# Strassen's seven block products for eight in the gate and up projections of the long sequence, with the stages in a new order and the residual gathered in DRAM

## The chip, the cores and the metric

The kernel runs on one core of one Trainium2 chip. The metric is the device time of an execution in microseconds; a lower time is better. The core has a matrix engine (TensorE, "PE" in the profile, with "PEld" for its weight loads), a vector engine (DVE), a scalar engine (ACT), a general engine (POOL) and a sync engine (SP). Work is kept in SBUF (on-chip memory, 128 partitions) and matmuls accumulate in PSUM banks, which hold 128 x 512 fp32 each. DMA queues move data between DRAM and SBUF; here SP issues the loads of weights, and POOL issues everything that is written to DRAM and read back.

## The reference, cut to what matters

One encoder layer is applied to a long sequence ("s", 1024 tokens) and a short one ("p", 512 tokens), each of width 1024, with the same weights. Per sequence a modulation vector scales and shifts the input of each of the three sub-layers:

```
mod = silu(c) @ w_ada + b_ada                      # 9 vectors of 1024: shift, scale, gate three times
hn = rmsnorm(x, ffn1_norm) * (1 + sc1) + sh1
x = x + 0.5 * g1 * swiglu(hn, w_gate, w_up, w_down)    # silu(hn @ w_gate) * (hn @ w_up) @ w_down
hn = rmsnorm(x, mix_norm) * (1 + sc2) + sh2
q, k, v, hy_in = split(hn @ w_in)
x = x + g2 * (concat(rmsnorm(attention(q, k, v)), rmsnorm(hyena(hy_in))) @ w_out)
hn = rmsnorm(x, ffn2_norm) * (1 + sc3) + sh3
x = x + 0.5 * g3 * swiglu(hn, w_gate2, w_up2, w_down2)
y = rmsnorm(x, final_norm)
```

The hidden width of each feed-forward network is 2816, 22 blocks of 128 columns. Attention is a neighbourhood attention over a grid 64 wide; hyena convolves the sequence with filters that a small network makes, once for each sequence length.

## The kernel before, in words

Activations are kept transposed: x of a sequence is a list of chunks of 512 tokens (`q.xT[c]`, two chunks for the long sequence, one for the short), each 8 tiles of 128 features by 512 tokens. Every matrix product is done in fp32r with both operands split into a high half (a copy rounded to fp32r, on ACT) and a low half (the rest, on DVE), and three terms: high by high, low by high, high by low. `mm` (L130) issues a matmul, `load_unit` (L347) loads a 512 KB piece of weights and splits it into halves, `col_unit` (L360) does so for one block of 128 columns.

`ffn` (L519) is a feed-forward network. It goes over 11 groups of two column blocks. For a column block it makes gate and up of each chunk, 8 k-tiles x 3 terms = 24 matmuls of 128x512 for each of the two; ACT takes silu, DVE multiplies, and the product is split into halves again. `down` then multiplies the two blocks by their rows of w_down: 8 output tiles of 6 matmuls for each chunk. DVE adds each output tile, times the gate, into x, which stays in SBUF. For the long sequence that is 192 + 96 = 288 matmuls a group, for the short one 144, with six loads of 512 KB in both cases.

The order of the work is set by `merge` (L1224). It takes a main stream (matrix products) and a side stream (filters, hyena, attention), and lets the side stream advance in step with the main one, by counters of TensorE and DVE work, against totals in the table `PLAN`. Operations of the main stream are recorded at L116 and of the side stream at L118, DMAs at L152 (SP) and L155 (POOL). The stages are:

- A: the first network of the long sequence, with the filters of the long sequence, the rest of the modulation vectors (`ada_rest`, 24 loads of 1 MB into `wada6a` and `wada6b`) and the filters of the short sequence as side work
- C: the projection of the long sequence, the first network and the projection of the short one, with the hyena and the attention of the long sequence as side work
- E: the output projection and the second network of the long sequence, with the attention and hyena of the short one, and its output projection, as side work
- last, the second network of the short sequence alone

Names in the profile: `gu`, `dn` and `mx` are PSUM banks (3, 2 and 3 of them), `hl` halves of weights, `raw` the weights as loaded, `act` activations, `s` and `a` small tiles of 128x512 (two buffers each), `hn1h` and `hn1l` the halves of the modulated input, `xTs` or `xRs` the resident x of the long sequence, `xscr_s` its place in DRAM, `mscA` and `mscB` scratch, `qscr`, `kscr`, `hscr` and `vscr` places in DRAM.

Of the kernel before, what the change touches and what calls it, by code (L numbers as in the profile page):

```python
# [17 lines left out]
P = 128  # L18
# [74 lines left out]
def build(ctx, tc, nc, A):  # L93
# [107 lines left out]
    for qn, L in SEQ_LEN.items():  # L201
# [5 lines left out]
        q.C = L // 512  # L207
        q.x = A[f"x_{qn}"]
# [389 lines left out]

    def proj_v(q, hn):

        vv = q.vscr.rearrange("(a b) c -> b a c", b=q.R)
        for cc in range(2):
# [6 lines left out]
            for b in range(q.R):  # L609
# [13 lines left out]
    def proj_qk(q, hn, part, hps, dst=None):  # L623
# [11 lines left out]
        for c in range(q.C):  # L635
# [31 lines left out]
    def proj_hy(q, hn, bk):  # L667
# [5 lines left out]
        for c in range(q.C):  # L673
# [258 lines left out]
    def hyena(q, ar, mc):  # L932
# [11 lines left out]
        for cb in range(NCB):  # L944
# [34 lines left out]
            for c in range(q.C):  # L979
# [3 lines left out]
                if mc is None:  # L983
                    se.copy(x[:, c * 512:(c + 1) * 512], ps)
                else:
                    se.copy(mc[c][4 + cb], ps)
            if mc is None:
                dmb(q.mscr[cb], x)
# [190 lines left out]
    class Final:  # L1179
# [6 lines left out]
        def add(self, c, kt):  # L1186
# [4 lines left out]
            if kt == 0 and self.q is Pq:  # L1191
                se.activation(warm, self.sq[c].acc[:, 0:1], AF.Sqrt)
# [75 lines left out]
    xr = [slices(i, "xr", F32) for i in (6, 7)]  # L1268
    rs = []
# [7 lines left out]
    def x_in(c, get):  # L1277
        ss = t_st()
        load_x(S, c, c, blk(2 + c, [P, 4, 1024], F32, "xin"), ss, junk, get)
        rs.append(rstd_rows(rstd_cols(ss, D)))  # L1280

    def x_scale(c, kts):
        for kt in kts:
            tt(xr[c][kt], S.xT[c][:, kt], rs[c], ALU.mult)
    x_in(0, gu)
    x_scale(0, range(KT))
# [3 lines left out]
    x_in(1, dn)  # L1290
    hn1 = [hn_pair(2, 3, "hn1"), hn_pair(4, 5, "hn1")]
    norm_pre(S, hn1, 0, xr[0], lo4)
    filS = filters(S, 7, *mixed_msc())

    def begin1():
        sums = [(gu(), gu()), (gu(), dn())]
        gemm_along(sums[0], w0, *hn1[0], lo4)
        x_scale(1, lo4)
        norm_pre(S, hn1, 1, xr[1], lo4)
        gemm_along(sums[1], w0, *hn1[1], lo4)  # L1300
        x_scale(1, hi4)
        ada_half(1, get_ring)
        norm_pre(S, hn1, 0, xr[0], hi4)
        gemm_along(sums[0], w0, *hn1[0], hi4)
        norm_pre(S, hn1, 1, xr[1], hi4)
        gemm_along(sums[1], w0, *hn1[1], hi4)
# [19 lines left out]
    hn2 = []  # L1326

    def after1(c, sq):
        hn2.append(hn_pair(2 + 2 * c, 3 + 2 * c, "hn2"))
        norm_mod(S, 1, hn2, c, sq)  # L1330

    side = chain(filS, ada_rest, lambda: filters(Pq, 7, *mixed_msc()))
# [18 lines left out]
    def s_attention():  # L1351
        kT = [blk(i, [P, 4, 1024], F32R, "kTs") for i in (4, 5)]
        for i in range(2):
            for h in range(4):
                dmb(kT[i][:, h], S.khl[4 * i + h])
# [203 lines left out]
```

## Time and profile before

| | us |
|---|---|
| median of 3 runs | 3217.09 (3212.54 to 3219.84) |
| the profiled execution, its own time | 3219.08 |
| span of the profile, first to last instruction | 3217.2 |
| TensorE busy | 3167.9 |
| DVE busy | 1940.6 |
| ACT busy | 1082.3 |
| POOL busy | 237.5 |

The profiled execution is one execution on the chip. A busy time is the union of an engine's instructions; a group's own busy time can count overlapping instructions apart, so that the mean of a matmul in a group is longer than the time from one matmul to the next. "Idle before" is the time in which the engine stood still just before an instruction of the group, and the arrow says what ended that.

### The profile page before, as it was taken

The numbers are of one execution on the slowest core, as the hardware profiler recorded it, in microseconds if no ns is written. First come the engines' busy times: TensorE is split into PE (matmuls) and PEld (weight loads), VectorE is DVE, ScalarE is ACT, GpSimd is POOL, SyncE is SP. The second block draws the span as 40 slices with busy tenths as digits, with TensorE's granted clock in tenths as the row PEclk, the third lists the DMA queues.
The fourth block names the chain that finished last, engine by engine and source line by source line (L and its number), as shares of the span: only waits on it lengthen the run. The fifth ranks groups of instructions, "written<-read, shape, count | busy, mean of one in ns | idle before, by whom it ended". The sixth has DMA issues, their size and how long they took to land.

```text
span 3217.2 us, 40525 instructions
## 1 busy us (share of the span) xinstructions
PE 3167.9 (98%) x15819; PEld 2592.3 (81%) x15819; DVE 1940.6 (60%) x3537; ACT 1082.3 (34%) x1964; POOL 237.5 (7%) x417
## 2 busy tenths in 40 slices
PE   7999999999999999999999999999999999999998
PEld 5788887778887889887777877788888888888887
DVE  5777653336784856987667468556554444654545
ACT  5211111112254333224666456411122222543233
POOL 1000030000111012001221000000000000000000
PEclk9999999999999999999999999999999999999999
DMA  7222154331354355434443444222111222343332
GB/s 263 88 78 78 55 171 162 131 124 54 89 173 138 124 151 180 168 111 145 127 131 123 151 137 136 84 63 76 58 58 46 66 85 85 118 131 99 99 95 76
DMA packets 320559, 364.09 MB, mean 113 GB/s; under 512 B 13536, under 2 KB 271736, under 8 KB 313488
## 3 DMA queue, kind: packets, MB, share of 16 engines
q1 hardware_dynamic: 287808, 232.81, 23.6%
q0 software_dynamic: 32528, 128.69, 12.5%
q8 instruction: 124, 2.03, 0.3%
q14 instruction: 67, 0.55, 0.1%
q10 hardware_dynamic: 32, 0.01, 0.0%
HBM read 310.33 MB, written 60.51 MB: 115 GB/s over the span
## 4 chain that ended last, share of the span: by engine, by line
PE 90%; issue 4%; DVE 2%; DMA 2%; ACT 1%; POOL 0%; SPq 0%; DVEq 0%; POOLq 0%; ACTq 0%
PE gu L130 56%; PE dn L130 20%; PE mx L130 13%; PE mx L134 1%; PE dn L134 1%; DVE r L118 1%; DMA xin<-in_x_s 0%; DMA mscA<-qscr_s 0%; DVE fT6b L118 0%; DMA mscr_s<-hyz6b 0%; DVE fA6a L118 0%; DMA raw<-in_w_in 0%; PE gu L134 0%; DMA fT6b<-in_zt_p 0%; DMA raw<-in_ffn_w_up 0%
## 5 line engine op out<-in xcount | busy, mean ns | idle before, releaser
L116 ACT ACTIVATE hl<-raw 128x512 fp32r<-128x512 f32 x680 | 427.6, 631 | 1023.3 <-PE gu L130 476.9
L116 DVE TENSOR_TENSOR hl<-raw,hl 128x512 fp32r<-128x512 f32 x680 | 465.2, 689 | 460.8 <-ACT hl L116 458.4
L130 PE MATMUL dn<-act,hl 128*128 128x512 f32 x2904 | 695.0, 393 | 3.5 <-DVE xTp L116 3.5
L130 PEld LDWEIGHTS dn<-act,hl 128*128 128x128 f32 x2904 | 539.1, 188 | 130.2 <-issue 5.7
L130 PE MATMUL gu<-hn3h,hl 128*128 128x512 f32 x1408 | 438.9, 392 | 0.0
L130 PE MATMUL gu<-hn1h,hl 128*128 128x512 f32 x1392 | 434.5, 392 | 0.8 <-ACT hn1h L116 0.8
L130 PEld LDWEIGHTS gu<-hn1h,hl 128*128 128x128 f32 x1392 | 258.1, 188 | 67.5 <-issue 9.1
L130 PEld LDWEIGHTS gu<-hn3h,hl 128*128 128x128 f32 x1408 | 262.9, 188 | 56.8 <-issue 3.4
L116 DVE TENSOR_TENSOR a<-s,gu 128x512 f32<-128x512 f32 x131 | 90.0, 687 | 331.1 <-PE gu L130 331.1
L130 PE MATMUL gu<-hn3l,hl 128*128 128x512 f32 x704 | 274.7, 390 | 0.0
L130 PE MATMUL gu<-hn1l,hl 128*128 128x512 f32 x696 | 271.5, 390 | 0.0
L130 PE MATMUL gu<-hn1ph,hl 128*128 128x512 f32 x704 | 224.9, 394 | 1.1 <-DVE hl L116 1.1
L130 PE MATMUL gu<-hn3ph,hl 128*128 128x512 f32 x704 | 217.4, 389 | 0.0
L130 PE MATMUL gu<-hn2h,hl 128*128 128x512 f32 x640 | 201.6, 395 | 2.8 <-ACT hl L116 2.6
L116 ACT ACTIVATE s<-gu 128x512 f32<-128x512 f32 x132 | 79.0, 598 | 340.6 <-PE gu L130 340.4
L116 DVE SCALAR_TENSOR_TENSOR xTs<-dn,Gc_s,xTs 128x512 f32<-128x512 f32 x176 | 131.5, 749 | 53.4 <-PE dn L130 52.6
L116 DVE SCALAR_TENSOR_TENSOR xRs<-dn,Gc_s,xRs 128x512 f32<-128x512 f32 x176 | 131.7, 749 | 45.3 <-PE dn L130 44.9
L130 PEld LDWEIGHTS gu<-hn3l,hl 128*128 128x128 f32 x704 | 132.2, 188 | 27.7 <-issue 0.5
L130 PEld LDWEIGHTS gu<-hn1ph,hl 128*128 128x128 f32 x704 | 130.9, 188 | 29.0 <-issue 2.6
L130 PEld LDWEIGHTS gu<-hn3ph,hl 128*128 128x128 f32 x704 | 132.1, 188 | 27.5
L130 PEld LDWEIGHTS gu<-hn1l,hl 128*128 128x128 f32 x696 | 130.7, 188 | 29.0 <-DVE hn1l L116 0.8
L116 ACT ACTIVATE act<-a 128x512 fp32r<-128x512 f32 x132 | 83.4, 632 | 193.6 <-DVE a L116 190.5
(393 smaller groups left out, 4553.1 us busy)
## 6 DMA issues: line engine op xcount, KB each, us to landing
raw<-in_ffn_w_gate SPq DMA_DIRECT2D x92, 512.0 KB, 4.0
raw<-in_ffn_w_up SPq DMA_DIRECT2D x92, 512.0 KB, 4.0
raw<-in_ffn_w_down SPq DMA_DIRECT2D x92, 512.0 KB, 3.5
raw<-in_w_in SPq DMA_DIRECT2D x48, 512.0 KB, 4.2
wada6b<-in_w_ada SPq DMA_DIRECT2D x12, 1024.0 KB, 4.9
wada6a<-in_w_ada SPq DMA_DIRECT2D x12, 1024.0 KB, 4.9
raw<-in_w_out SPq DMA_DIRECT2D x24, 512.0 KB, 4.2
kscr_s<-fA6a POOLq DMA_DIRECT2D x8, 1024.0 KB, 4.6
```

The costliest lines, as they stand in the source:

```text
L116: return fn(*a, **k)
L118: r = fn(*a, **k)
L130: nc.tensor.matmul(out, lhsT, rhs, start=start, stop=stop)
L134: nc.tensor.transpose(out, in_, idn)
```

## The change

- `Fast` and `Pair` do gate and up of the long sequence with Strassen's scheme (in Winograd's form) over 2 x 2 blocks: two column blocks of the weights, two halves of the 1024 features, two chunks of tokens. Seven products of 512 features replace eight, `PRODUCTS` lists them. `A` blocks are the weights, `S` blocks sums of them (made anew in each group, on DVE); `B` blocks are activations, `T` blocks sums of them (made once for a network, when `need` first asks).
- `ffn_fast` runs a network of the long sequence with these. A PSUM bank goes on accumulating after ACT has copied its value out, so that the intermediate sums come out of the bank.
- In `down`, all groups but the last send their output tile to DRAM: ACT multiplies it by the gate into a tile `s` or `a`, and a DMA with an addition (`accum_op`) adds it to `xscr_s`. The x of the long sequence is no longer resident in a network; the last group reads it back and adds on DVE as before.
- The stages are in a new order. A: the first network and the projection of the short sequence, with the filters, `ada_rest` and the input of the long sequence (`s_input`) as side work. Then the first long network alone. C: the long projection, with attention and hyena of the short sequence. D: the output projection and second network of the short sequence, with hyena and attention of the long one. Then the long output projection and the second long network, alone.
- The short attention takes q and k as halves in fp32r, as the long one did, for fp32 before.

The core of the diff:

```diff
-    def mm(out, lhsT, rhs, start, stop):
+    def mm(out, lhsT, rhs, start, stop, resume=False):
         work["pe"] += size(rhs) * (0.42 if rhs.dtype == F32R else 1.68)
-        nc.tensor.matmul(out, lhsT, rhs, start=start, stop=stop)
+        nc.tensor.matmul(out, lhsT, rhs, start=start, stop=stop, skip_group_check=resume)
...
+    PRODUCTS = (("A11", "B11"), ("S1", "T1"), ("S2", "T2"), ("A12", "B21"), ("S3", "T3"), ("S4", "B22"),
+                ("A22", "T4"))
...
+        def need(self, nm):
+            if nm in self.T:
+                return
...
+            for i in range(4):
+                if nm == "B11":
+                    self.scale(0, i)
+                    self.split(nm, i, z1[i], self.b1[i])
+                elif nm == "T1":
+                    self.scale(1, i)
+                    tt(z1[i], z2[i], z1[i], ALU.subtract)
+                    self.split(nm, i, z1[i], None)
...
+        def weights(self, nm):
+            a, t = self.A, self.tmp
+            if nm == "S1":
+                tt(t, a["A21"], a["A22"], ALU.add)
+                h = self.halves(t)
+                tt(a["A21"], a["A11"], a["A21"], ALU.subtract)
+                tt(a["A11"], t, a["A11"], ALU.subtract)
+                a["S3"], a["S2"] = a["A21"], a["A11"]
+                return h
...
+        def product(self, n, T):
+
+            b = self.banks
+            (wh, wl), (th, tl) = self.weights(PRODUCTS[n][0]), T
+            to, start = ((0, True), (2, True), (0, False), (1, True), (0, False), (2, False), (0, False))[n]
+            if b[to] is None:
+                b[to] = self.get()
+            for i in range(4):
+                mm(b[to], wh[i], th[i], start and i == 0, False, not start)
+                mm(b[to], wl[i], th[i], False, False, not start)
+                mm(b[to], wh[i], tl[i], False, i == 3, not start)
+            k = self.keep
+            if n == 0:
+                se.copy(k[0], b[0])
+            elif n == 1:
+                se.copy(k[3], b[2])
+            elif n == 2:
+                se.copy(k[1], b[0])
+            elif n == 3:
+                tt(k[0], k[0], b[1], ALU.add)
+            elif n == 4:
+                se.copy(k[2], b[0])
+                tt(k[2], k[2], k[3], ALU.add)
+            elif n == 5:
+                tt(k[1], k[1], b[2], ALU.add)
...
+            G = Pair(wg, f0, [t_raw(), t_raw()], mA[:, 1024:1536], [None] * 3, keeps[0])
+            U = Pair(wu, f0, [t_raw(), mB], mA[:, 1024:1536], [None] * 3, keeps[1])
+            G.get, U.get = gu, mx
+            for n, (_, b) in enumerate(PRODUCTS):
+                fast.need(b)
+                for pr in (G, U):
+                    pr.product(n, fast.T[b])
+                if end and n < 2:
+                    if n == 0:
+                        q.xT = []
+                    reload_x(q, n, xblocks[n])
+                yield
...
+                    if end:
+                        xv = q.xT[c][:, dt]
+                        stt(xv, ps, gain, xv, ALU.mult, ALU.add)
...
+                    else:
+                        y = (t_s, t_a)[dt % 2]()
+                        se.activation(y, ps, AF.Copy, scale=gain)
+                        nc.gpsimd.dma_start(q.xscr[c][:, dt * 512:(dt + 1) * 512], y, accum_op=ALU.add)
...
+    merge("A", p_front(), chain(filters(Pq, 7, *mixed_msc()), ada_rest,
+                                lambda: filters(S, 7, *mixed_msc()), s_input))
...
+    run(ffn_fast(S, fast[0], A["ffn1_w_gate"], A["ffn1_w_up"], A["ffn1_w_down"], 0, after1, None, 7, (0, 5)))
...
+    merge("C", s_proj(), p_mixer())
...
+    merge("D", p_back(), s_mixer())
...
+        if c == 0:
+            fast.append(Fast(S, 2, z3, rows3, {"B11": 0, "T1": 1, "T2": 4, "B21": 6, "T3": 2, "B22": 3, "T4": 5}))
+            for nm in ("B11", "B21"):
+                fast[1].need(nm)
...
+    run(ffn_fast(S, fast[1], A["ffn2_w_gate"], A["ffn2_w_up"], A["ffn2_w_down"], 2, None,
+                 Final(S, any_ps, lambda c, b: t_act()), 7, (0, 1)))
...
-PLAN = {"A": (976e3, 446e3, 0.0, 0.92), "C": (952e3, 413e3 + 40e3, 0.0, 0.94), "E": (1116e3, 250e3 + 15e3, 0.0, 0.93)}
+PLAN = {"A": (726e3, 509e3, 0.0, 0.94), "C": (321e3, 176e3, 0.0, 0.94), "D": (586e3, 413e3, 0.0, 0.94)}
```

The order of TensorE in the first long network, before: gate of one column block, in runs of three terms for each k-tile, with matmuls of the filters (`mx<-mscA`) between them.

```order
L130 MATMUL gu<-hn1l_391,hl 128x512
L130 MATMUL gu<-hn1h_390,hl 128x512 x2
L130 MATMUL gu<-hn1l_391,hl 128x512
L130 MATMUL mx<-mscA 128x256 x12
L130 MATMUL gu<-hn1h_392,hl 128x512
L130 MATMUL mx<-mscA 128x256 x4
L130 MATMUL gu<-hn1h_392,hl 128x512
L130 MATMUL gu<-hn1l_393,hl 128x512
```

The same network after, where one group ends and the next begins: the seventh product of up, down in one block, and the first products of gate (`gu`) and up (`mx`) in turn.

```order
L130 MATMUL mx<-T46a,hl 128x512 x2
L130 MATMUL mx<-T46b,hl 128x512
L130 MATMUL dn<-act,hl 128x512 x96
L130 MATMUL gu<-B_5534,hl 128x512 x12
L130 MATMUL mx<-B_5534,hl 128x512 x12
L130 MATMUL gu<-T_5596,hl 128x512 x12
```

Nothing of the side streams stands between them any more, and a product takes 12 matmuls for the 24 of a column block before.

The additions of down in the same network, on DVE, before: `xTs_153` and `xTs_317` are the two chunks of x.

```order
L116 TENSOR_TENSOR act<-a,act 128x512
L116 SCALAR_TENSOR_TENSOR xTs_153<-dn,Gc_s,xTs_153 128x512 x8
L116 SCALAR_TENSOR_TENSOR xTs_317<-dn,Gc_s,xTs_317 128x512 x3
L116 TENSOR_TENSOR hl<-raw,hl 128x512
L116 SCALAR_TENSOR_TENSOR xTs_317<-dn,Gc_s,xTs_317 128x512
L116 TENSOR_TENSOR hl<-raw,hl 128x512
```

The same work on ACT after, in the second half of one group's down; `Gc_s` is the gate, and `hl<-mscA` and `hl<-raw` are weight halves of the next group.

```order
L116 ACTIVATE s<-dn,Gc_s 128x512
L116 ACTIVATE a<-dn,Gc_s 128x512
L116 ACTIVATE s<-dn,Gc_s 128x512
L116 ACTIVATE hl<-mscA 128x512
L116 ACTIVATE a<-dn,Gc_s 128x512
L116 ACTIVATE hl<-mscA 128x512
L116 ACTIVATE s<-dn,Gc_s 128x512
L116 ACTIVATE a<-dn,Gc_s 128x512
```

On POOL a row `L805 DMA xscr_s<-s 128x512` or `xscr_s<-a` follows for each of them, 16 in a row for a group. With its waits shown, a copy from the fifth of a group on waits for one of the semaphores of those DMAs, that of the DMA four before it.

The loads of the modulation weights on SP, in stage A, before:

```order
L152 DMA raw<-in_ffn_w_gate 128x8x128
L152 DMA wada6b<-in_w_ada 128x2048
L152 DMA wada6a<-in_w_ada 128x2048
L152 DMA wada6b<-in_w_ada 128x2048
L152 DMA wada6a<-in_w_ada 128x2048
L152 DMA wada6b<-in_w_ada 128x2048
L152 DMA wada6a<-in_w_ada 128x2048
L152 DMA raw<-in_ffn_w_up 128x8x128
L152 DMA raw<-in_ffn_w_gate 128x8x128
```

And after, where the last of a longer run stand, ahead of the next load of up:

```order
L152 DMA wada6b<-in_w_ada 128x2048
L152 DMA wada6a<-in_w_ada 128x2048
L152 DMA wada6b<-in_w_ada 128x2048
L152 DMA wada6a<-in_w_ada 128x2048
L152 DMA wada6b<-in_w_ada 128x2048
L152 DMA wada6a<-in_w_ada 128x2048
L152 DMA raw<-in_ffn_w_up 128x8x128
```

Twelve of these loads now stand in a row where six did, and the gate and up loads around them are those of the short sequence.

## Rows read from the trace of the kernel before

**Rows 1.** The page: busy us (share of the span) and instructions.
```profile
PE 3167.9 (98%) x15819; PEld 2592.3 (81%) x15819; DVE 1940.6 (60%) x3537; ACT 1082.3 (34%) x1964; POOL 237.5 (7%) x417
```
**Rows 2.** The page: shares of the chain that ended last, by engine and line.
```profile
PE 90%; issue 4%; DVE 2%; DMA 2%; ACT 1%; POOL 0%; SPq 0%; DVEq 0%; POOLq 0%; ACTq 0%
PE gu L130 56%; PE dn L130 20%; PE mx L130 13%; PE mx L134 1%; PE dn L134 1%; DVE r L118 1%; DMA xin<-in_x_s 0%; DMA mscA<-qscr_s 0%; DVE fT6b L118 0%; DMA mscr_s<-hyz6b 0%; DVE fA6a L118 0%; DMA raw<-in_w_in 0%; PE gu L134 0%; DMA fT6b<-in_zt_p 0%; DMA raw<-in_ffn_w_up 0%
```
**Rows 3.** Waits of TensorE, whole span: us in total, times, longest.
```profile
PE mx L130 <- DVE r L118: 5.3, 5, 1.3
PE dn L134 <- DMA xin<-in_x_s: 5.0, 2, 4.3
```
**Rows 4.** Windows: length, busy us (instructions) by engine, TensorE clock, DMA share, GB/s.
```profile
core 0: us, PE busy (x) PEld busy (x) DVE busy (x) ACT busy (x) POOL busy (x), PEclk, DMA share, GB/s
0.00:43.00 43.00, 25.44 (x156) 16.86 (x157) 17.86 (x48) 24.09 (x44) 12.44 (x28) 0.84 0.96 326
...
20.00:30.00 10.00, 3.64 (x52) 1.58 (x44) 7.65 (x19) 2.31 (x5) 1.77 (x3) 0.74 0.95 291
30.00:40.00 10.00, 8.69 (x42) 6.42 (x42) 3.60 (x9) 6.94 (x13) 0.00 (x0) 0.58 1.03 348
500.00:700.00 200.00, 200.00 (x932) 146.12 (x932) 72.66 (x110) 31.95 (x52) 0.55 (x1) 1.00 0.44 148
...
1290.00:1450.00 160.00, 160.00 (x803) 134.79 (x802) 144.52 (x247) 45.91 (x76) 6.25 (x12) 1.00 0.42 138
```
**Rows 5.** The chain, pieces: start us, us, engine, line, instructions.
```profile
1212.06 46.08 PE gu L130 x384
...
2079.05 21.88 PE dn L130 x96
...
2115.39 32.66 PE gu L130 x144
```
**Rows 6.** Groups, shapes apart: busy us, mean ns, idle before and its releaser.
```profile
L116 DVE TENSOR_TENSOR hl<-raw,hl 128x512 fp32r<-128x512 f32 x680 | 465.2, 689 | 460.8 <-ACT hl L116 458.4
...
L116 ACT ACTIVATE hl<-raw 128x512 fp32r<-128x512 f32 x680 | 427.6, 631 | 1023.3 <-PE gu L130 476.9 <-PE dn L130 399.6 <-issue 86.0
...
L116 DVE SCALAR_TENSOR_TENSOR xTs<-dn,Gc_s,xTs 128x512 f32<-128x512 f32 x176 | 131.5, 749 | 53.4 <-PE dn L130 52.6
...
L116 ACT ACTIVATE s<-gu 128x512 f32<-128x512 f32 x132 | 79.0, 598 | 340.6 <-PE gu L130 340.4
...
L130 PE MATMUL mx<-qkP 64*128 64x256 f32 x64 | 18.7, 428 | 0.0
```
**Rows 7.** DMA issues: number, KB each, us to landing.
```profile
kscr_s<-fA6a POOLq DMA_DIRECT2D x8, 1024.0 KB, 4.6
...
qscr_s<-act POOLq DMA_DIRECT2D x16, 256.0 KB, 7.3
...
hscr_p<-act POOLq DMA_DIRECT2D x12, 256.0 KB, 2.4
mscB<-hscr_p POOLq DMA_DIRECT2D x10, 256.0 KB, 3.1
...
vwin_s<-vscr_s POOLq DMA_DIRECT2D x4, 8.0
```
**Rows 8.** One name's instructions: ns min/median/max, first and last start.
```profile
L155 POOL DMA_DIRECT2D hscr_p<-act x12: 542/542/563, 1835.7 to 1920.4; - x12
```
**Rows 9.** Windows, side work (L118) alone: busy us by engine, clock, DMA.
```profile
1000.00:1480.00 480.00, 212.67 (x379) 13.75 (x25) 1.00 0.45 145
```

More of the change, by code (lines that the diff above doesn't have):

```diff
@@ L207, in build @@
         q.C = L // 512
+        q.cs = (1, 0) if q.C == 2 else (0,)
         q.x = A[f"x_{qn}"]
@@ L634, in proj_qk @@
             outs = [dst[:, hp] for hp in hps]
-        for c in range(q.C):
+        for c in q.cs:
             pss = [gu() for hp in hps]
@@ L672, in proj_hy @@
         u, acc = t_act((P, R, P)), t_act((P, R, P))
-        for c in range(q.C):
+        for c in q.cs:
             ps = gu()
@@ L982, in hyena @@
                     tr(ps[:, bb * P:(bb + 1) * P], zv[:, 4 * c + bb], ident)
[L983 to L988, printed above, removed]
+                se.copy(mc[c][4 + cb], ps)
             yield
@@ L1324, in ada_rest @@
             ada_gain(k)
[L1326 to L1332, printed above, removed]
-    merge("A", ffn(S, hn1, A["ffn1_w_gate"], A["ffn1_w_up"], A["ffn1_w_down"], 0, after1, gate1,
-                   begin=begin1), side)
-    spill_x(S)
-    def s_hyena():
-        fm = blk(0, [P, 4096], F32, "hyF")
-        at = blk(1, [P, 4096], F32, "hyA")
-        kk = blk("6a", [P, 2048], F32, "hyK")
-        zx = blk("6b", [P, 2048], F32, "hyz")
-        m, m2 = msc()
-        yield from hyena(S, dict(F=fm[:, 0:2048], M=fm[:, 2048:4096], A=at[:, 0:2048], T=at[:, 2048:4096],
-                                 K=kk, z=[zx[:, 0:1024], m[:, 0:1024]], x=zx[:, 1024:2048]), None)
-        S.mcH = [blk(i, [P, 2, 1024], F32, "mcH") for i in ("6a", "6b")]
-        for i in range(2):
-            dmb(S.mcH[i], S.mscr[2 * i:2 * i + 2].rearrange("h p t -> p h t"))
@@ new lines, in build @@
+    mxP = []
+    def p_mixer():
+        kT = blk(7, [P, 8, 512], F32R, "kTp")
+        for h in range(8):
+            dmb(kT[:, h], Pq.khl[h])
+        w = blk(0, [P, 4096], F32, "atP")
+        m, m2 = mixed_msc()
+        mc = slices(6, "mcP", F32)
+        ar = dict(bias=[w[:, 0:1024], w[:, 1024:2048]], V=w[:, 2048:2560], E=[w[:, 2560:2816], w[:, 2816:3072]],
+                  PT=[w[:, 3072:3328], w[:, 3328:3584]],
+                  q=[w[:, 3584:3840], m[:, 0:256], m[:, 256:512]])
+        yield from attention(Pq, None, [kT[:, 0:4], kT[:, 4:8]], ar, [mc])
+        w = blk(5, [P, 4096], F32, "hyP")
@@ L1502, in build @@
+    g = out_proj(S, mxS[0], 0, after3)
+    next(g)
+    next(g)
+    mxS.append(hn_pair(2, 3, "mxs"))
+    run(mix_norm(mcS[1], *mxS[1]))
+    reload_x(S, 1, 5)
+    run(g)
+    run(out_proj(S, mxS[1], 1, after3))
     nps = [0]
```

386 lines of the change are left out of this document (238 added, 148 removed).

## The prediction

> **What bounds the kernel now.** I read the profile from the whole to the parts: busy time by engine, the chain that ended last, the waits of TensorE, tables of windows, single pieces of the chain, and last the groups by operation and the DMA issues.
>
> TensorE is busy 3167.9 us of the 3217.2 us span [rows 1], and the chain by engine gives it 90%, with 4% "issue" (time that waits for nothing the profile shows) and DVE, DMA and ACT at 1 to 2% each [rows 2]. The longest single waits of TensorE are 5.3 and 5.0 us in total [rows 3]: no other engine holds it up in a way that adds up. Two windows show how robust that is. In the densest stretch of DVE, from 1290 to 1450 us, DVE is busy 144.52 of 160 us and TensorE still 160.00; with DMA at a share of 0.44, from 500 to 700 us, TensorE is busy 200.00 of 200 [rows 4]. So a DVE at 90% and a DMA at 44% cost this kernel nothing, and time is saved only by giving TensorE less to do. The one exception is the start: 25.44 busy us in the first 43, with DMA at 0.96 and 326 GB/s [rows 4].
>
> A matmul of 128 x 512 in fp32r takes 32.66/144 = 0.2268 us in gate and up and 21.88/96 = 0.228 us in down; one with 256 columns 46.08/384 = 0.120 us [rows 5]. These are taken from the chain, because the mean of a group counts overlapping matmuls twice.
>
> **The change part by part.**
>
> **Gate and up of the long sequence.** Per pair of 128-column blocks, 192 matmuls become 7 products x 4 k-tiles x 3 terms x 2 matrices = 168. Over 11 pairs and two networks 24 x 22 = 528 go: 528 x 0.2268 = -119.8 us. All of it lay on the path, since TensorE had no gaps there. Down keeps its 96 matmuls per pair. A bank that takes a second product must first be copied out by ACT, 0.60 us (its silu of that shape, 0.598 [rows 6]); at least three other products of 12 matmuls, 8.2 us, lie between and cover it. Should that cover fail at each of the four such copies of a matrix, 22 pairs lose up to 8 x 0.60 us each, 106 us; I take nothing.
>
> **Scores of the short attention.** They were fp32, 64 rows with 18.7 us busy [rows 6]; now they are 64 fp32r matmuls of 256 columns, 64 x 0.120 = 7.7 us: -11.0 us. The extra split of q and k is ACT and DVE work beside TensorE.
>
> Together -130.8 us. What follows can only take away from that.
>
> **Down's result goes to DRAM.** Before, each of the 16 tiles of a pair was added into resident x by one DVE instruction of 0.749 us [rows 6]. Now ACT copies it to one of four tiles and an accumulating DMA of 256 KB on POOL's queue adds it to x in DRAM; only the last pair of each network still adds on DVE. That is 20 pairs x 16 = 320 DMAs. Each ACT copy waits for the DMA four before it, as the order with its waits shows. TensorE makes a tile in 6 x 0.228 = 1.367 us, so four tiles last 5.47 us. One use of a tile costs the copy 0.60 us, POOL's issue 0.54 us [rows 8] and the landing L. It is free up to L = 5.47 - 1.14 = 4.3 us. Beyond that, the first four copies of a pair find free tiles and 12 wait, so a pair loses 12 x ((L + 1.14)/4 - 1.367) us. Behind the waiting copy stand, on ACT, the next pair's weight splits, and behind down's two banks TensorE itself; both wait.
>
> No row shows an accumulating DMA. Lower end of L: a plain write of 256 KB, 2.4 us [rows 7], no loss, and no gain either, since DVE's additions were hidden. Between: write plus read back, 2.4 + 3.1 = 5.5 us [rows 7], which gives 12 x 0.293 = 3.5 us a pair, +70 us. Scaled from DRAM to DRAM, 8.0 us for `vwin_s` (1 MB by its tiles) against 4.6 for 1 MB written from SBUF [rows 7], L = 2.4 x 1.74 = 4.2 us, no loss. Upper end: 8.0 us, the slowest nearby row, 12 x 0.918 = 11.0 a pair, +220 us; a plain 256 KB write has taken 7.3 us where others queued before it [rows 7]. I take L = 4.7 us, between the ratio and the sum and a little nearer the ratio: 12 x 0.093 = 1.1 a pair, **+22 us** over 20.
>
> The Trainium skill, "DMA: Bandwidth & Descriptors", section "Anatomy of one DMA — SWDGE (gpsimd) path", gives a DMA of POOL's queue about 2.0 us plus its bytes at 436 GB/s. For 256 KB that makes 2.6 us, where the trace has 2.4, and the trace's 7.3 us for the same size under load disagrees with it. With both streams counted, 512 KB, it would be an estimated 3.2 us and no loss at all: 3117 us in place of the forecast.
>
> **Long networks alone on the chip.** They have no side work now, so DVE and ACT are free for the splits: per pair 14 + 8 weight halves, 8 sums of weights, 6 additions of products and 8 for the activation, 44 x 0.689 = 30.3 us of DVE beside 264 x 0.228 = 60 us of TensorE. That is hidden. Not so in the first pair of the second network: there the transformed x must be made as well, 44 instructions (scale, subtract, split) of 0.69 to 0.75 us, 31.7 us, plus 28 x 0.689 = 19.3 for the weights: 51 us of DVE beside 168 x 0.2268 = 38.1 us of TensorE. 13 us late by that, 15 with the wait of the first product, and nothing if the splits of the first blocks start beside the projection's end: 0 to +15, taken **+8**. In the first network most of that is made as side work of the stage before.
>
> **Side work beside the short sequence.** The filters, both hyenas and the long attention now run beside less TensorE work. In the order I priced every DVE row by the mean of its form [rows 6] over steps of 40 us of TensorE work: the fullest hold 48, 43.8 and 42.5 us, in the long hyena of stage D (side work 212.67 us of DVE, before spread over 480 us [rows 9]) and in the long filters of stage A. Excess 8 + 3.8 + 2.5 = 14 us. None of it if neighbouring steps take it up; 40 if DVE never catches up over the 320 us in which it has about as much work as TensorE (an eighth of them). Taken **+10**.
>
> **The modulation weights.** SP's order puts twelve loads of 1 MB in a row where gate and up loads stood between them, and the short sequence needs 3 MB of weights for every 144 matmuls, 32.7 us. Over some 120 us I count 38 MB, 315 GB/s, close to the 326 GB/s at share 0.96 of the start, where TensorE starved [rows 4]; before, the same loads ran at 148 GB/s from 500 to 700 us [rows 4]. From nothing (if the lead of the loads carries it) to 25 us late (eight of the twelve, 8 MB at 326 GB/s, ahead of a load that TensorE needs at once). Taken **+10**.
>
> **Start and seams.** The kernel starts with one chunk of x, 2 MB, for two, but with half as many matmuls to cover the modulation weights; three stages end where two products must be final before the next can begin. -8 (a little under half of the 17.6 idle us of the first 43 [rows 4]) to +12, taken **+3**.
>
> Sum: -130.8 + 22 + 8 + 10 + 10 + 3 = -77.8 us, against the profiled execution's 3219.1 us: 3141.3. The median of the runs is 2.0 us below that execution: **3139 us**.
>
> **The rivals.**
> - *The accumulations decide (slower).* At L = 6.0 us the 20 pairs lose 99.8 us and the change is worth nothing; at the 7.3 us of a loaded write [rows 7] they lose 178 and the time is 3295 us, at 8.0 us 3337. For: the four megabytes of a pair are read and written in DRAM inside 22 us, 190 GB/s each way, while the next weights load. Against: the unloaded writes of this size are far from it. Gaps could also lower TensorE's clock: it was granted 0.74 and then 0.58 in the two windows in which TensorE had been busy 3.64 of 10 us [rows 4], and a block of down, 21.88 us, would take 16 us more at 0.58. The Trainium skill, "TensorE: Matmul & The Clock Gate", section "HAM oscillation — how this bites in real kernels", says the same of bursts with waits between them; the trace of the start agrees with it.
> - *Side work or a moderate L decide.* L = 5.5 gives 3187 us; DVE at +40 to +50 in place of +10 gives 3169 to 3179. For: DVE's full steps above. Against: the 144.52 of 160 us that cost nothing [rows 4].
> - *Nothing is lost.* 3219.1 - 130.8 - 2.0 = 3086 us. For: the present kernel hides everything. Against: three places where the working above finds more than an engine can hold.
> - *No difference.* The losses eat the gain by chance, 3211 to 3223.
>
> **How the numbers follow.** Within 0.2% is 6.4 us, about what a measurement of this kernel can tell from no change. Forecast (3105 to 3165) 0.44; nothing lost 0.13; side work or moderate L (3165 to 3210) 0.18; no difference 0.04; accumulations decide 0.21. So faster 0.75, same 0.04, slower 0.21. The likeliest case's own range is 3105 to 3165. The range of 8 in 10 starts at the nothing-lost case, 3085, and reaches into the slower one, to 3235, where some 0.16 is left above.
>
> **What would show it.** TensorE's busy time falls by some 125 us; in the long networks the chain is TensorE through gate and up, and inside down it has short waits for ACT, whose copies wait for DMAs of `xscr_s`. Their landing time in the list of issues decides most: 4.7 us would be right, 4.3 and less the nothing-lost case, 6 and more the slower rival, with a granted clock below 1.00 in those stretches. In the first pair of the second long network TensorE should wait some 8 us for DVE; beside the long hyena for DVE and in stage A for `raw` loads behind `wada6a` and `wada6b`. I am wrong if TensorE waits mainly elsewhere, or if its own matmuls take longer than 0.227 us while their clock is full.

## The result and the profile after

The changed kernel takes 3313.10 us (3309.11 to 3316.80, median of 4), before 3218.47 us in the same comparison: a ratio of 1.0297, 95% interval 1.0277 to 1.0317. It is slower by 95 us; 3139 us with a range to 3235 had been forecast. The time is near that of the rival "the accumulations decide" (3295 us), but by luck: that rival put 178 us on the accumulations, and they turn out to cost only about 52.

The page after: busy us, share of the span, instructions. It answers to [rows 1].

```profile
span 3313.8 us, 41364 instructions
PE 3116.6 (94%) x15283; PEld 2512.2 (76%) x15283; DVE 2012.5 (61%) x3720; ACT 1440.1 (43%) x2606; POOL 548.7 (17%) x809
```

TensorE is busy 51 us less, where some 125 had been forecast, and its idle time has grown from 49 us (3217.2 - 3167.9) to 197 (3313.8 - 3116.6). The mean granted clock is 0.976 for 0.994. Span times the missing share gives 80 us for 19: at most some 60 us more are lost to the lower clock (at most, since a slow stretch can also hold idle time), and that is the main reason why the busy time fell so little. So the loss is of two kinds, gaps and stretches of slow clock after them.

The waits of TensorE after (us in total, times, longest), where [rows 3] had two of 5 us at the head:

```profile
PE dn L130 <- ACT a L116: 18.3, 31, 2.0
PE gu L130 <- DVE hl L116: 15.8, 7, 9.8
PE dn L130 <- ACT s L116: 13.9, 31, 1.1
PE mx L130 <- DVE r L118: 13.3, 15, 1.8
PE dn L130 <- DVE r L118: 12.0, 2, 8.4
PE mx L130 <- DMA wada6b<-in_w_ada: 8.8, 4, 6.6
```

The first and the third are down waiting for its copies, as forecast. The copies in turn wait for the DMAs, by the waits of ACT:

```profile
ACT s L116 <- DMA xscr_s<-s: 82.3, 80, 2.0
ACT a L116 <- DMA xscr_s<-a: 82.1, 92, 2.8
```

The other waits of TensorE lie almost all in the stages beside the short sequence. The windows after, by stage; the last two are one pair of the first long network, gate and up and then down, and the one before them is gate and up of the first pair of the second long network:

```profile
core 0: us, PE busy (x) PEld busy (x) DVE busy (x) ACT busy (x) POOL busy (x), PEclk, DMA share, GB/s
...
100.00:310.00 210.00, 190.99 (x1026) 147.96 (x1025) 122.19 (x225) 46.02 (x85) 39.58 (x68) 0.98 0.61 191
...
546.00:593.00 47.00, 36.53 (x192) 31.06 (x191) 38.34 (x67) 15.77 (x27) 2.68 (x5) 0.89 0.36 123
593.00:794.00 201.00, 182.88 (x1032) 156.20 (x1031) 157.03 (x308) 91.97 (x193) 44.94 (x83) 0.97 0.56 177
...
1864.00:1930.00 66.00, 58.58 (x302) 48.83 (x300) 56.40 (x105) 20.50 (x36) 3.66 (x7) 0.94 0.53 175
1930.00:2441.00 511.00, 485.53 (x2645) 394.99 (x2646) 418.08 (x895) 219.08 (x438) 76.22 (x125) 0.97 0.42 128
2441.00:2490.00 49.00, 33.10 (x131) 25.57 (x130) 39.01 (x72) 28.31 (x53) 0.00 (x0) 0.78 0.24 77
...
2588.55:2637.75 49.20, 42.70 (x179) 31.85 (x178) 45.81 (x78) 30.20 (x52) 0.53 (x1) 1.00 0.17 54
...
861.73:899.58 37.85, 37.85 (x168) 31.34 (x167) 21.27 (x32) 17.64 (x31) 2.18 (x3) 1.00 0.47 108
899.58:925.00 25.42, 23.33 (x98) 17.65 (x97) 5.46 (x9) 12.38 (x19) 11.91 (x14) 1.00 0.90 133
```

Gate and up of a pair run without a gap, 37.85 us for 168 matmuls, so the 0.2268 us of [rows 5] holds and the seven products do what they say. Down takes 25.4 us in this pair and 24.7 on average. The rest of the idle time lies before 794 us (stage A), in stage C and the seam behind it (20 us from 1487 to 1930), in stage D (1930 to 2490 us) and in the first pair of the second long network (from 2588.55 us, 49.2 us for 37.85).

The DMA issues and the issuing instructions of the accumulation (KB, us to landing; ns min/median/max), which answer to [rows 7, 8]:

```profile
xscr_s<-s POOLq DMA_DIRECT2D x160, 256.0 KB, 5.5
xscr_s<-a POOLq DMA_DIRECT2D x160, 256.0 KB, 5.4
```

```profile
L805 POOL DMA_DIRECT2D xscr_s<-s x160: 844/849/1292, 839.6 to 3231.3; - x160
```

An accumulation lands after 5.5 us and takes POOL 0.85 us to issue; 4.7 and 0.54 had been taken.

Last, one seam, from the timelines of DVE and of TensorE (start us, us, engine, line, instruction, idle before it). It is the norm between the short sequence's first network and its projection.

```profile
573.62 0.16 DVE L116 TENSOR_SCALAR st<-dn 128x4 f32<-128x4 f32 x1 [0.54 <-PE dn L130]
...
575.21 3.58 DVE L118 TENSOR_REDUCE r<-fT6b 128x128 f32<-128x2048 f32 x1
578.71 0.17 DVE L116 RECIPROCAL st<-st 128x4 f32<-128x4 f32 x1
```

```profile
572.52 1.05 PE L130 MATMUL dn<-ones,r 128*128 128x1 f32 x8 [2.65 <-DVE r L116]
578.93 0.77 PE L130 MATMUL mx<-r,ones 128*128 128x128 f32 x2 [5.36 <-DVE st L116]
...
579.78 9.47 PE L130 MATMUL mx<-fT6b,fF 128*128 128x128 f32 x64
589.08 1.02 PE L130 MATMUL dn<-a,ones 128*128 128x512 f32 x2
592.57 1.65 PE L130 MATMUL gu<-hn2ph,hl 128*128 128x512 f32 x6 [2.46 <-ACT hn2ph L116]
```

TensorE sums the squares, and then waits while the norm's few small DVE operations stand behind a side operation of 3.58 us. After that it is not idle but takes 64 matmuls of the filters (`mx<-fT6b,fF`), 9.47 us, and the norm's own last matmuls (`dn<-a,ones`) stand behind them; the projection can start only at 592.57. The short sequence has one chunk of 512 tokens, so no other chunk's matmuls lie in between.

### The profile page after: what moved, and what is told of

It is laid out like the page before. It is cut to its first block, busy times and chain, and to the rows that moved or that the text cites. A ratio compares the mean times of both kernels' runs of the same rounds, so it can differ in the third digit from the quotient of the medians.

```text
span 3313.8 us, 41364 instructions
## 1 busy us (share of the span) xinstructions
PE 3116.6 (94%) x15283; PEld 2512.2 (76%) x15283; DVE 2012.5 (61%) x3720; ACT 1440.1 (43%) x2606; POOL 548.7 (17%) x809
## 5 line engine op out<-in xcount | busy, mean ns | idle before, releaser
L805 POOL DMA_DIRECT2D xscr_s<-s x160 | 136.8, 855 | 872.8 <-ACT s L116 866.3
L130 PE MATMUL gu<-T,hl 128*128 128x512 f32 x924 | 225.3, 391 | 5.1 <-ACT T L116 2.8
L130 PE MATMUL mx<-T,hl 128*128 128x512 f32 x924 | 224.2, 390 | 0.0
L130 PEld LDWEIGHTS gu<-T,hl 128*128 128x128 f32 x924 | 172.8, 188 | 43.6 <-ACT T L116 4.3
L130 PEld LDWEIGHTS mx<-T,hl 128*128 128x128 f32 x924 | 173.3, 188 | 36.6 <-ACT act L116 0.4
L130 PE MATMUL gu<-B,hl 128*128 128x512 f32 x660 | 160.7, 391 | 1.2 <-DVE hl L116 1.2
L130 PE MATMUL mx<-B,hl 128*128 128x512 f32 x660 | 159.9, 391 | 1.8 <-ACT act L116 1.8
L805 POOL DMA_DIRECT2D xscr_s<-a x160 | 137.0, 856 | 112.6 <-ACT a L116 107.4
L130 PEld LDWEIGHTS mx<-B,hl 128*128 128x128 f32 x660 | 124.0, 188 | 28.3 <-ACT act L116 2.2
L130 PEld LDWEIGHTS gu<-B,hl 128*128 128x128 f32 x660 | 124.2, 188 | 27.5 <-DVE hl L116 1.7
```

The costliest lines, as they stand in the source:

```text
L130: nc.tensor.matmul(out, lhsT, rhs, start=start, stop=stop, skip_group_check=resume)
L805: nc.gpsimd.dma_start(q.xscr[c][:, dt * 512:(dt + 1) * 512], y, accum_op=ALU.add)
```

## The experiments

Times are medians of 4 (one of 2), each beside runs of the kernel before on the same chip, with the ratio to it and its 95% interval. The first four are edits of the changed kernel, except that the first also goes back in part.

**The order alone.** Both long networks call the old `ffn` again, with x resident; the stages stay in the new order.

```diff
-    run(ffn_fast(S, fast[0], ..., 0, after1, None, 7, (0, 5)))
+    run(ffn(S, hn1s, ..., 0, after1))
...
-    run(ffn_fast(S, fast[1], ..., 2, None, Final(S, ...), 7, (0, 1)))
+    run(ffn(S, hn3s, ..., 2, None, None, Final(S, ...)))
```

> The new order of stages and the fp32r attention scores are kept; both long networks go back to eight products with x resident in SBUF, so no sum of blocks, no copies of banks and no accumulating DMA. Theory 1 (most of the loss lies in the new order: the seams of the one-chunk sequence and the denser side work, with the lower clock after each gap): 3313 + 120 for the 528 matmuls that come back - 56 for down (20 pairs at 24.7 us for 21.9) - 15 for the first pairs = about 3360 us. Rival 2 (the accumulating DMAs and Strassen's first pairs cost the time and the order is free): 3218 - 11 = about 3207 us.

Measured: 3346.86 us, 1.0395 (1.0378 to 1.0411). That is 128 us above before, with 11 us of work less by the prediction's estimate of the scores: the new order alone costs about 139 us. Theory 1 holds and rival 2 falls. Idle time makes 92 us of that (142 us for 49; of the 142, 73 lie in stage A, 15 in C and 41 in D), and TensorE is busy 37 us more, at a clock of 0.978 for 0.994. Its windows, stage A's second part, the first long network, stage D and its end:

```profile
100.00:310.00 210.00, 193.29 (x1034) 148.44 (x1033) 123.89 (x228) 47.49 (x87) 39.62 (x68) 0.98 0.61 193
...
790.00:1507.00 717.00, 714.58 (x3141) 587.84 (x3139) 290.46 (x426) 155.60 (x255) 9.34 (x17) 1.00 0.20 62
...
1942.00:2451.00 509.00, 483.90 (x2647) 393.19 (x2648) 417.77 (x894) 219.89 (x439) 76.36 (x125) 0.98 0.43 129
2451.00:2506.00 55.00, 39.10 (x158) 31.77 (x157) 42.49 (x82) 31.12 (x58) 0.00 (x0) 0.76 0.22 74
```

The long network alone loses 2 us in 717. The stages beside the short sequence have the same gaps as in the changed kernel, with no accumulating DMA anywhere.

**More tiles for down's results.**

```diff
-                        y = (t_s, t_a)[dt % 2]()
+                        y = (t_s, t_a)[dt // 2 % 2]() if dt % 2 else spare.pop(0)   # spare: 8 slices of pp
```

> Down's results go through twelve tiles (the eight that keep the products, idle during down, and the four of before), each used again eight tiles later or in the next pair. Theory 1 (four tiles with a landing of 5.5 us and an issue of 0.85 us hold down up by 2.8 us a pair): down back to 21.9 us a pair, about 3313 - 56 = 3257 us; its reading in the trace is a down block of 96 matmuls without gaps. Rival 2 (DMA engines or DRAM are the limit of the accumulations, not the number of tiles): the waits come back eight tiles later, over 3295 us.

Measured: 3260.99 us, 1.0130 (1.0110 to 1.0150), 52 us less. Theory 1 holds. The windows of one pair (gate and up, down), and the DMA issue:

```profile
858.46:896.32 37.86, 37.86 (x169) 31.36 (x168) 21.29 (x32) 17.52 (x31) 2.21 (x3) 1.00 0.47 108
896.32:918.43 22.11, 22.09 (x98) 17.95 (x96) 5.46 (x9) 13.24 (x20) 12.15 (x15) 1.00 0.91 142
```

```profile
xscr_s<-pp POOLq DMA_DIRECT2D x160, 256.0 KB, 6.1
```

Down is back at 22.1 us although an accumulation now lands even later, 6.1 us: the number of tiles had been the limit, not the DMA engines.

**Plain writes.**

```diff
-                        nc.gpsimd.dma_start(q.xscr[c][...], y, accum_op=ALU.add)
+                        nc.gpsimd.dma_start(q.xscr[c][...], y)
```

> The DMAs of down write instead of adding; left out is the addition into x of all pairs but the last. Theory 1 (the landing of an accumulating DMA is what holds the tiles): landing falls from 5.5 us to 2.5 to 3 us, down back to 21.9 us a pair, about 3257 us. Rival 2 (any DMA of POOL's queue lands late beside the weight loads, or its issue of 0.85 us holds): landing over 4.5 us, over 3290 us.

Measured: 3256.59 us, 1.0115 (1.0097 to 1.0134). Its DMA issue and the issuing instruction:

```profile
xscr_s<-s POOLq DMA_DIRECT2D x160, 256.0 KB, 2.3
```

```profile
L805 POOL DMA_DIRECT2D xscr_s<-s x160: 539/540/545, 842.3 to 3172.8; - x160
```

At the same place and under the same loads a write lands in 2.3 us and an accumulation in 5.5; the addition costs 3.2 us of landing and 0.31 us of issue.

**Gaps filled with small matmuls.** At five seams TensorE multiplies constants in part of the gap.

```diff
-    def rstd_of(acc, n, ps=None):
-        return rstd_rows(rstd_tok(acc, n, (ps or dn)()), ps)
+    def rstd_of(acc, n, ps=None, sp=(0, 0, 0)):
+        spin(sp[0])            # so many fp32 matmuls of 128x128, ones by identity
+        r = rstd_tok(acc, n, (ps or dn)())
+        spin(sp[1])
...
```

> Small matmuls on constants fill some of the gaps of TensorE at the seams of the short sequence and at the end of stage D, about as long as each gap was; nothing else changes. Theory 1 (after a gap TensorE runs at 1.2 GHz for 7 to 17 us, and that is some 59 us more than before over the whole kernel): the four stretches at half clock at 574, 1922, 2444 and 2485 us shrink, 10 to 25 us saved: 3288 to 3303 us. Rival 2 (what follows the gaps waits for DVE anyway, so a full clock gives nothing): 3313 us within 5.

Measured: 3302.38 us, 1.0259 (1.0236 to 1.0283), 10.7 us less, at the lower edge of theory 1; the mean clock rose from 0.976 to 0.982. The windows of three of the seams:

```profile
546.00:593.00 47.00, 44.69 (x274) 38.92 (x273) 40.76 (x73) 16.08 (x28) 2.68 (x5) 1.00 0.36 124
1864.00:1930.00 66.00, 64.97 (x365) 55.98 (x364) 59.86 (x111) 21.04 (x35) 3.12 (x6) 1.00 0.50 162
2441.00:2490.00 49.00, 44.85 (x245) 37.95 (x244) 38.65 (x74) 27.80 (x51) 0.55 (x1) 0.97 0.30 100
```

The clock is 1.00 where it was 0.89 and 0.94, and 0.97 where it was 0.78, and no work that counts was taken away: the slow clock is a second price of the gaps. It is paid back only in part; that what follows a gap also waits for DVE (rival 2) is likely, but not shown.

The next seven start from the kernel with twelve tiles (3261 us) and change only the pace of the side work or its distance from the main stream.

**Stage D levelled.** Hyena's steps count 1.4 times in `merge`.

```diff
-        yield from hyena(S, dict(...), mc)
+        yield from slowed(hyena(S, dict(...), mc), 1.4)
-"D": (586e3, 413e3, 0.0, 0.94)
+"D": (586e3, 507e3, 0.0, 0.94)
```

> The kernel with twelve tiles, and in stage D the long hyena advances as if each of its steps were 1.4 times the work, so that it spreads over some 66% of the stage for 57% and the attention takes the rest. Theory 1 (in stage D TensorE waits because hyena's DVE work, at 48 to 50 busy us of 50, stands ahead of the low halves of the main stream's weights): DVE falls to some 85% there, the 9.8 us wait for hl and the slow clock after it go, 10 to 20 us saved: 3241 to 3251 us. Rival 2 (the waits in D are the single chunk's own chain of the norm and do not depend on DVE's load): within 4 us of 3261.

Measured: 3267.41 us, 1.0145 (1.0130 to 1.0161). It is 6 us slower than twelve tiles alone, which neither forecast has; the theory as I had put it falls.

**A longer and a shorter distance of side work.**

```diff
-LAG = 300
+LAG = 900        # in the other run 100
```

> The kernel with twelve tiles, and the operations of side streams are given 900 places of delay in the order in place of 300, so that on every engine the main stream's operations stand further ahead of them. Theory 1 (at the seams and in stage D the main stream's short operations on DVE stand behind long side operations): fewer gaps, 10 to 30 us saved, 3231 to 3251 us. Rival 2 (side work then meets its own deadlines later and TensorE, which takes side matmuls in order, waits for them): slower than 3261 us.

> As with 900, but 100 places. Theory 1: side operations stand closer to the front and the gaps grow, 3265 to 3290 us. Rival 2 (the distance costs by holding side results back): faster than 3261 us. No change would say that the distance does not decide where DVE is full.

Measured: 3272.58 us, 1.0156 (1.0139 to 1.0173) with 900 and 3255.04 us, 1.0109 (1.0094 to 1.0124) with 100; twelve tiles alone had 1.0130. Both forecasts of theory 1 are wrong, and rival 2 has the direction of both, with 100 places by 6 us and with intervals that overlap. The windows of stage D, its body and its end, with twelve tiles alone, levelled, and with 900:

```profile
1902.00:2408.00 506.00, 483.26 (x2646) 393.04 (x2647) 417.79 (x895) 218.97 (x438) 76.21 (x125) 0.98 0.43 129
2408.00:2463.00 55.00, 39.10 (x158) 31.67 (x157) 42.32 (x81) 31.05 (x58) 0.00 (x0) 0.76 0.28 93
```

```profile
1900.00:2370.00 470.00, 456.61 (x2444) 373.37 (x2444) 393.05 (x802) 190.03 (x371) 62.99 (x105) 0.99 0.43 128
2370.00:2471.00 101.00, 69.64 (x361) 52.15 (x360) 66.44 (x172) 56.21 (x121) 13.07 (x21) 0.77 0.34 103
```

```profile
1902.00:2357.00 455.00, 448.55 (x2380) 367.69 (x2380) 388.44 (x775) 178.41 (x345) 56.80 (x94) 0.99 0.43 129
2357.00:2483.00 126.00, 88.12 (x428) 65.03 (x427) 75.23 (x202) 66.17 (x144) 19.61 (x31) 0.72 0.31 96
```

In the body, which is shorter in the last two, the order on DVE does matter: idle time falls from 23 us to 13 and 6. But the side work left over then runs at the end of the stage as a chain of small operations over DVE, ACT and TensorE, in which TensorE is busy 70% at a clock of 0.72 to 0.77. With 900 places it runs with nothing beside it: the last block of down of the main stream stands behind it in TensorE's order.

```profile
2445.80 23.73 PE L130 MATMUL dn<-act,hl 128*128 128x512 f32 x96
```

The whole stage grows, 561, 571 and 581 us.

**An earlier end for the side work.** With 900 places, side work is also paced to end earlier; in three forms.

```diff
-LAG = 300
+LAGS = {'A': 300, 'C': 900, 'D': 900}   # d72: only D 900; a80: A and D 900
-"C": (321e3, 176e3, 0.0, 0.94), "D": (586e3, 413e3, 0.0, 0.94)
+"C": (321e3, 176e3, 0.0, 0.80), "D": (586e3, 413e3, 0.0, 0.80)   # d72: only D, 0.72; a80: A and D, 0.80
```

> The kernel with twelve tiles; stages C and D have 900 places between side and main operations in place of 300, and their side streams are paced to end at 0.80 of the main stream in place of 0.94, so that the longer distance leaves no tail of side work behind it. Theory 1 (in stage D the main stream waits for its short DVE operations behind side operations, 32 us, and the tail of side work has nothing beside it, 29 us; each of the runs before cured one of the two and worsened the other): both shrink, 3215 to 3245 us. Rival 2 (DVE has too much to do in the stage in any order): the gaps come back inside the stage, 3255 us or more.

> As the run before, for stage D alone, paced to end at 0.72. Theory 1: as good as 0.80 in the tail but hyena is squeezed: 3220 to 3250 us. Rival 2: 3260 us or more.

> Stages A and D with 900 places and a pace of 0.80, C as before. Theory 1 (stage A's gaps after 540 us, 51 us with the slow clock, are of the same kind): 10 to 25 us less than with stage D alone. Rival 2 (stage A's gaps are the single chunk's own chain of the norm, the loads of modulation weights and the input of the long sequence, which the distance does not touch): within 6 us of stage D alone, or slower because the filters squeeze the loads together.

Measured: 3305.43 us, 1.0271 (1.0252 to 1.0289); 3323.65 us, 1.0320 (1.0299 to 1.0340); 3337.37 us, 1.0368 (1.0351 to 1.0384). All are worse, against theory 1, and within what rival 2 gave in each. In the first of them, the second half of stage D:

```profile
2300.00:2450.00 150.00, 108.75 (x516) 78.67 (x515) 74.83 (x224) 68.47 (x157) 31.02 (x49) 0.68 0.29 88
```

From 2300 to 2450 us DVE is only half busy and TensorE waits all the same. By the timeline it has side matmuls alone from 2304 to 2422 us, and 75 us of the main stream follow. So it is not DVE's load that sets this stretch but the length of the side stream's own chain, with the matrix work that could cover it standing behind it in the order.

**The loads of modulation weights spread.**

```diff
-            yield 3000.0
+            yield 5500.0      # and 569e3 for 509e3 in PLAN["A"]
```

> The kernel with twelve tiles, and in stage A the 24 loads of modulation weights are spread over 1.5 times the work of the main stream. Theory 1 (the 19 us of gaps and 5 us of slow clock between 100 and 310 us come from loads at 320 GB/s): 8 to 15 us of them go, less what the filters lose by being closer together, 3246 to 3258 us. Rival 2 (the filters that follow are squeezed and lose as much as the loads gain): 3261 us or more.

Measured: 3270.01 us, 1.0152 (1.0133 to 1.0170); the gaps between 100 and 310 us did not shrink (187.82 us busy of 210 there, 191.53 with twelve tiles alone). The time is that of rival 2, but the run does not decide about the loads, since it hardly spread them: the 24 loads start over 164 us (230.28 to 393.85) for 133 (229.20 to 361.99) in the changed kernel, the first twelve as close together as there, and TensorE waits 14.6 us for them, for 12.3.

**Cover given back.** From the kernel with the order alone: the long filters move from stage A to the first long network.

```diff
-                                lambda: filters(S, 7, *mixed_msc()), s_input))
+                                s_input))
...
-    run(ffn(S, hn1s, ..., 0, after1))
+    merge("F", ffn(S, hn1s, ..., 0, after1), filters(S, 7, *mixed_msc()))
...
-"A": (726e3, 509e3, 0.0, 0.94)
+"A": (726e3, 294e3, 0.0, 0.80), "F": (969e3, 211e3, 0.0, 0.85)
```

> The new order with eight products (as in the first run of that name), but the long filters are side work of the first long network, which in the new order has none, and no longer of stage A. Theory 1 (the new order loses time because 1350 us of the long networks stand alone and all side work is packed beside the short sequence): stage A's gaps and slow clock fall by 25 to 50 us, the first long network stays without gaps although it now has side work: 3295 to 3325 us against 3347. Rival 2 (stage A loses its time to the single chunk, which no other chunk covers, and to the start): within 10 us of 3347.

Measured: 3316.69 us, 1.0305 (1.0290 to 1.0320), 30 us less than the order alone. The same stretch of stage A, and the first long network with the filters beside it:

```profile
100.00:310.00 210.00, 204.71 (x1081) 165.70 (x1080) 134.68 (x240) 54.22 (x97) 36.00 (x62) 1.00 0.57 172
...
668.00:1469.00 801.00, 796.15 (x3823) 663.48 (x3821) 435.61 (x692) 171.30 (x284) 27.38 (x48) 1.00 0.23 73
```

The gaps fall from 17 to 5 us in this stretch, those of all of stage A from 73 to 43, and the long network hides the filters with 5 us of idle time in 801. The time is the one of theory 1. But part of it belongs to the loads: with fewer side operations in the stage `PLAN` paces the rest more slowly, the 24 loads of modulation weights start over 226 us (223.73 to 450.13) for 132 (227.79 to 359.48) with the order alone, and the waits of TensorE for them fall from 9.7 to 1.1 us. The run does not separate these some 9 us from the cover.

**Side work taken away.** From the kernel with twelve tiles.

```diff
-    merge("A", p_front(), chain(filters(Pq, ...), ada_rest, lambda: filters(S, ...), s_input))
+    merge("A", p_front(), chain(ada_rest, s_input))
...
-        yield from attention(S, None, kT, ar, mcS)
+        ve.memset(mcS[c][k], 1.0)          # likewise for both hyenas and the short attention
```

> The kernel with twelve tiles without the work of the filters, of both hyenas and of both attentions: these are left out and constants stand in their place; the modulation weights, the input of the long sequence and all matrix products remain. Theory 1 (density of side work): in stages C and D next to no gaps remain, in stage A only those of the start. Rival 2 (single chunk): at the seams of the short sequence, between its first network and its projection and between its output projection and its second network, 10 and 8 us of gaps and 5 and 4 us of slow clock remain as they were. The two may share: the runs give each its part.

Measured: 2832.19 us. Stage A's body, its seam and stage D's body:

```profile
310.00:434.00 124.00, 124.00 (x566) 94.51 (x565) 56.70 (x93) 37.66 (x68) 0.00 (x0) 1.00 0.43 136
434.00:482.00 48.00, 34.85 (x162) 26.52 (x160) 34.79 (x83) 27.93 (x68) 9.31 (x18) 0.93 0.68 220
...
1660.00:2000.00 340.00, 339.90 (x1485) 279.27 (x1486) 171.57 (x251) 107.43 (x175) 0.00 (x0) 1.00 0.31 94
```

Without side work the bodies have next to no gaps (in stage C 2 us in 234), and the seam still has 13 us. Of these 7.9 lie around the norm, where the changed kernel has 10.5, and 5.2 before it, in the last block of down. Both theories have a part. The seam behind the output projection cannot be compared: the writing of the constants and the norm of the long mixer fall into it here.

**The parts together.** Twelve tiles, 100 places, and the filled gaps.

> Twelve tiles, 100 places of distance and the filled gaps together. If the parts add up: 3313 - 52 - 8 - 11 = about 3242 us, still slower than before by 0.7%. If the filled gaps were worth something only while down was held up: 3255.

Measured: 3250.45 us, 1.0103 (1.0087 to 1.0120): the parts do not add up fully, 8 us are missing. No version tried that does all the work beats the kernel before.

## Why the prediction was wrong

**What was right.** The removal of matmuls (gate and up without a gap at the forecast length), the place where down waits, its form (copies that wait for DMAs), and the first pair of the second long network (gate and up take 49 us for 38, 11 late; +8 taken, 15 as the bound). The prediction also named the sign of being wrong that came: TensorE waits mainly elsewhere. Of its 197 us of idle time only some 38 lie in the two long networks (in the windows from 794 to 1487 and from 2646 to 3269 us).

**Down's result goes to DRAM: +22 taken, 52 measured.** The mechanism was right and the size was off: landing 5.5 for 4.7 us, an issue of 0.85 for 0.54 us and a copy of 0.69 for 0.60 us. The value that I had worked out from write plus read back, 2.4 + 3.1 = 5.5 us [rows 7], was the right one. The formula with the measured numbers overstates it, (5.5 + 0.85 + 0.69)/4 = 1.76 us a tile and 94 us in all; the two PSUM banks may take up some, which it left out, but no run shows that. On the Trainium skill, "DMA: Bandwidth & Descriptors", section "Anatomy of one DMA — SWDGE (gpsimd) path": by its line an accumulation would have been an estimated 3.2 us with both streams counted; the trace disagrees, with 5.5 us, while the plain write, 2.3 us, is near its 2.6.

**Side work, loads, start and seams: +23 taken, about 139 measured.** This is the step that failed, and it decided the sign. I priced side work by busy time, DVE's fullest steps of 40 us against TensorE's, and found 14 us too much; I gave the start and the seams +3 and a slow clock beside the short sequence nothing. Two of the terms came out near: TensorE waits 12.3 us for the loads of modulation weights (+10 taken; it is their own matmuls that wait, not gate and up behind them), and in stage D, behind a stretch in which the hyena keeps DVE busy 194.5 of 200 us (1980 to 2180 us), TensorE waits 9.8 us for a weight half from DVE (+10 taken for all side work). The runs show three things in the place of the rest.
- *Cover.* Before, side work ran beside nearly all of the 2829 us up to the last network. Now the two long networks, some 1420 us, stand alone, since their blocks of sums fill SBUF, and the same side work runs beside the rest. What that does is seen at a network of the short sequence with the long hyena and attention beside it. In the kernel before that is the first network of the short sequence:

```profile
1261.00:1703.00 442.00, 437.26 (x2309) 357.38 (x2308) 326.49 (x679) 194.84 (x374) 66.45 (x110) 1.00 0.48 148
```

  There 180 us of DVE side work stand beside it, and TensorE is idle 5 of 442 us. In the changed kernel it is the second, in stage D (the row from 1930 us above): 269 us of DVE side work, and TensorE is idle 25 of 511 us. The 144.52 of 160 us of DVE that cost nothing [rows 4] lie in that first network, so a single chunk with dense side work need not lose; I took the row for a property of DVE's load, and did not ask how much more side work would stand there. Besides the rows, the filters moved back show this part (30 us, some 9 of them with the loads), and the run without side work (next to no gaps in the bodies). The pace and distance runs moved the loss to the end of the stage or made it larger.
- *Single chunk.* At the seams of the short sequence no other chunk's matmuls cover the norm. It costs 10 us of gaps and 5 of slow clock after its first network, and 7.9 us of the gaps remain when all side work is gone. The kernel before has this seam too, in the middle of stage C, and loses less there, 4.5 us of gaps and 5 of slow clock, by the window over it:

```profile
1702.00:1750.00 48.00, 43.48 (x243) 33.79 (x241) 38.99 (x99) 29.21 (x64) 10.79 (x17) 0.89 0.46 147
```

  The windows over the three seams after, from 546, 1864 and 2441 us, hold 34 us of gaps and 20 of slow clock (the last one with the side stream's own norm in it), and the first 100 us cost some 12 more than before (74.89 us busy at a clock of 0.85, for 78.37 at 0.93). Less the seam before, that makes some 56 us by these windows for the term start and seams, taken as +3.
- *The clock.* A gap is paid twice: after it TensorE runs for a while at the lower of its two levels, 1.2 for 2.4 GHz. Behind the wait of 9.8 us in stage D, for one, a matmul of 128x512 takes 0.43 us for 0.227. At the start this stood in the rows ([rows 4], 0.74 and 0.58), and I gave it to the slower rival for down alone, whose short waits leave the clock at 1.00 (the pair from 861.73 us). It came through the gaps beside the short sequence, at most some 60 us, which are part of the parts above. On the Trainium skill, "TensorE: Matmul & The Clock Gate", section "HAM oscillation — how this bites in real kernels": its rule, that gaps between bursts bring the lower clock, agrees with the trace, clock 0.89 and 0.78 at the seams and 1.00 and 0.97 with the gaps filled.

**The sum.** Against before: +128 for the order with its cheaper scores (139 - 11), -120 for the matmuls of gate and up, +52 for down, which makes +60. The other 35 us to the measured 95 can be placed by the first matmul of each stage, against the run with the order alone: 4 us before the first long network, 10 in that network beyond matmuls and down, 10 in the stage behind it, and 13 in the second long network, of which 11 are gate and up of its first pair. What causes the first three was not looked into.

**Still open.** How cover, clock, start and seams share the 139 us exactly. The runs give 30 us for the long filters, loads included, and 10 to 16 us for a seam; for stage D there are only the rows above and the run without its side work. That the matrix work which is left could cover the side work in some other order is not ruled out: the pace was varied, but the last blocks of the main stream stood behind the side stream in the slow runs.

## What to carry to other kernels

A step that saves matrix work but needs the memory or the time in which other work ran beside it takes its cover away; count how much side work must now run beside each stretch of matrix work (here 269 us of DVE beside 511 us, for 180 beside 442), what is left over at its end, and what stands behind it in the order. A row in which a full engine cost nothing holds for the mix of that stretch. Price a new gap of TensorE twice, once as idle time and once as slow clock after it. An accumulating DMA needs more buffers than a plain one of the same size: here four tiles were too few and twelve were enough, where four sufficed for the plain write.

## What was not expected of the hardware

An accumulating DMA of 256 KB from SBUF to DRAM took 5.5 us to land where the plain write took 2.3, and 0.85 us of POOL's time to issue for 0.54. With more of them under way it landed later, 6.1 us, and its throughput was still enough for a tile every 1.37 us.
